# GpSimd arithmetic taken out of the routing, and the last residual spread over the experts on VectorE

## The chip, the cores and the metric

The kernel runs on one core of a Trainium2 chip. The time is the device time of one execution in microseconds (us). A core has five engines with a queue each, which run their own instructions in order and wait for each other through semaphores: TensorE (PE in the profile, its weight loads PEld), VectorE (DVE), ScalarE (ACT), GpSimd (POOL) and SyncE (SP, which only issues transfers here). TensorE's clock has two levels, 2.4 and 1.2 GHz; the profile prints the granted clock as a share of the higher one.

## The reference, cut to what matters

256 tokens of width 1024 pass a two-layer decoder: RWKV-7 time mixing and a dense SwiGLU, then dilated attention and a top-2-of-8 mixture of experts. All that matters here is the end of layer 1:

```python
def post_norm(t, y, l, j):
    gate = sub_mod[:, l, j, 2][:, None, :]
    return layer_norm(DEEPNORM_ALPHA * t + (1.0 + gate) * y, ln_g[l, j], ln_b[l, j])
...
x = post_norm(x, dilated_attention(h, k_sh, v_sh, ...), 1, 0)   # norm 1, 0
h = modulate(x, shift, scale)
top_logit, top_idx = lax.top_k((h @ router), 2)                 # routing
y = sum over experts e of  weight_e * (silu(h_e @ w_gu[e, :, :3584]) * (h_e @ w_gu[e, :, 3584:])) @ w_down[e]
x = post_norm(x, y, 1, 1)                                       # norm 1, 1
```

Each expert has 44 MB of float32 weights (1024 x 7168 and 3584 x 1024), 352 MB for all eight.

## The kernel before, in words

Tokens lie in two tiles `t` = 0 and 1 of 128 rows. Nearly all instructions come from one helper (line 191), so that a row of the profile is told apart by its tiles.

**Precision.** Every float32 weight is split in two float32r parts. `split` copies `raw` to `whi` on ScalarE (`SC.copy`) and takes `wlo = raw - whi` on VectorE; PE then makes three products a block (`mm3`: `whi` and `wlo` with the high part of the activations, `whi` with the low part). One split is 128 x 1024 elements and feeds six matmuls of 512 columns. `whi` and `wlo` have a ring of four buffers each, so ScalarE and VectorE can be up to three splits ahead of the one that PE reads. The first `GPM` splits of the experts run on GpSimd in place of VectorE: `e = GP if cnt[0] <= gp_to[0] else V`, with `gp_to[0] = cnt[0] + GPM`.

**Weights.** SP issues the loads of `raw` (1 MB each, 12 places that rotate; the first pass has a few extra places in tiles that are free by then: `lngb`, `lnbb`, `u`, `gate1`, `acc`). Loads 14, 17 and 18 (`OGP`) go through GpSimd's queue. A place is loaded again once `whi` and `wlo` have been taken from it. A line of `ln_g` or `ln_b` is loaded into `lngb` or `lnbb`, repeated on all partitions (`ln_rows`, `bcast_row`).

**Norm 1, 0 and routing** (`out_task(t)`, one for each tile). The attention's output is projected (`psb<-whi,oh` and so on), `pn_norm` makes `u = layer_norm without its row factors` on VectorE: product with the gate, residual, statistics (`bnst`, `bnmv`), a Newton root in tiny 128x1 steps (`ln_v`, `ln_i`, `ln_y`, `ln_a`), and two halves of `u`. PE transposes `u`, the modulated copy `modtmp` goes through the router (`mmb<-rt,modtmp`, 128x8), and about twenty tiny VectorE steps find the two largest logits, `oh` and `M` (one-hot), and the weights `Wt`. When both tiles are there, `route_task` counts the ranks (`mmb<-M,cnt_w`), makes the permutation `P` on VectorE, gathers the tokens of expert 0 with `P` on PE (`psb<-P,hn`), and the experts begin. At the end of `out_task` GpSimd computes the norm's row factors for the residual, which is needed much later: `yield from pn_res(t, u, pre3["gb"], pre3["bb"], GP)`, two 128x1024 products, `u<-u,lngb` and `xres<-u,lnbb`. `keep_clock2` puts dummy matmuls (`identr`) on PE where a planner at build time expects PE to wait. The order of this part is written by that planner (`spin`, from costs for each engine); in the experts the framework orders the instructions.

**Experts** (`run_experts`). Expert `i` has seven steps `j`: gate half, the down projection of the step before, up half. `macc[t]` collects the weighted outputs. In the last expert, after step 2, `moe_hook` lets GpSimd compute `macc*gate`, `xres*alpha` and their sum, so that after `fin` only the last expert's own part, the statistics and the last row factors remain.

Of the kernel before, what the change touches and what calls it, by code (L numbers as in the profile page):

```python
# [24 lines left out]
F32 = mybir.dt.float32  # L25
# [3 lines left out]
AF = mybir.ActivationFunctionType  # L29
OP = mybir.AluOpType  # L30
AX = mybir.AxisListType

D = 1024
S = 256
DFF = 2816
NE = 8
DFFE = 3584
KAPPA = math.exp(-0.5)
ALPHA = math.sqrt(2.0)
# [52 lines left out]
def tile_kernel(ctx: ExitStack, tc: tile.TileContext, cst_d, att_d, x, c, ada_w, ada_b, ln_g, ln_b, mu, w_rkv,  # L92
# [18 lines left out]
    def load(t_, src):  # L111

        n = 1
        for d_ in t_.shape:
            n *= d_
        k = t_.tensor.name
        clk["DMA"] = max(clk["DMA"], free.get(k, 0.0)) + n * 4 / 360
        rdy[k] = clk["DMA"] + 2000
        (nc.gpsimd if k in by_gp else SY).dma_start(t_, src)
# [74 lines left out]
    V, SC, GP, PE = Engine(nc.vector, "V"), Engine(nc.scalar, "SC"), Engine(nc.gpsimd, "GP"), Engine(nc.tensor, "PE")  # L194
# [216 lines left out]
    def bg_until(idx):  # L411
        while idx not in mods:
            bg_step()

    def bcast_steps(idx, o, get_ps):

        for hf in range(2):
            yield PE, mods[idx]
            ps = get_ps()
            for i in range(4):  # L420
                k = hf * 4 + i
                PE.matmul(ps[:, i * 128:(i + 1) * 128], mods[idx][:, k:k + 1].to_broadcast([128, 128]), ident,
                          start=True, stop=True)
            yield SC, ps
            SC.copy(o[:, hf * 512:(hf + 1) * 512], ps)

    def bcast_mod(idx, pool):
        bg_until(idx)
        o = pool.tile([128, D], F32, name="gate1", bufs=1)
        for _ in bcast_steps(idx, o, pst):  # L430
            pass
        return o
# [20 lines left out]
    def bcast_row(t, src):  # L453
        load(t, bass.AP(tensor=src.tensor, offset=src.offset, ap=[[0, 128], [1, t.shape[1]]]))
# [69 lines left out]
    def ln_rsqrt(var):  # L524

        v, i, y, a = (small.tile([128, 1], I32 if n == "i" else F32, name="ln_" + n, bufs=2) for n in "viya")
        yield V, var
        V.tensor_scalar(v, var, LN_EPS, -0.5, op0=OP.add, op1=OP.mult)
        yield V, v
        V.tensor_scalar(i, v.bitcast(I32), 1, None, op0=OP.logical_shift_right)  # L530
        yield V, i
        V.tensor_scalar(y.bitcast(I32), i, -1.0, float(0x5f3759df - (1 << 22) + (1 << 30)), op0=OP.mult, op1=OP.add)
        for _ in range(3):
            yield V, y
            V.scalar_tensor_tensor(a, y, v, y, op0=OP.mult, op1=OP.mult)
            yield V, a
            V.scalar_tensor_tensor(y, a, 1.5, y, op0=OP.add, op1=OP.mult)
        return y

    def pn_norm(t, yps, gate1, u, sc=(), g_=None):  # L540

        st = small.tile([128, 2, 6], F32, name="bnst", bufs=2)
        for hf in range(2):
            csl = slice(hf * 512, (hf + 1) * 512)
            yield V, yps[hf], gate1
            g = u if g_ is None else g_
            V.tensor_tensor(g[:, csl], yps[hf], gate1[:, csl], op=OP.mult)
            yield V, g, xres[0]
            V.scalar_tensor_tensor(u[:, csl], xres[0][:, t, csl], ALPHA, g[:, csl], op0=OP.mult, op1=OP.add)
            yield V, u  # L550
            V.bn_stats(st[:, hf], u[:, csl])
        mv = small.tile([128, 2], F32, name="bnmv", bufs=2)
        yield V, st
        V.bn_aggr(mv, st)
        rs = yield from ln_rsqrt(mv[:, 1:2])
        if sc:
            nm = mv[:, 1:2]
            yield V, rs
            V.scalar_tensor_tensor(nm, mv[:, 0:1], -1.0, rs, op0=OP.mult, op1=OP.mult)
        for hf in range(2):  # L560
            csl = slice(hf * 512, (hf + 1) * 512)
            if hf in sc:
                yield SC, nm
                SC.activation(u[:, csl], u[:, csl], AF.Identity, scale=rs, bias=nm)
            else:
                yield V, rs
                V.tensor_scalar(u[:, csl], u[:, csl], mv[:, 0:1], rs, op0=OP.subtract, op1=OP.mult)
# [21 lines left out]
    def pn_res(t, u, gb, bb, eng):  # L589

        yield eng, u, gb
        eng.tensor_tensor(u, u, gb, op=OP.mult)
        yield eng, u, bb
        eng.tensor_tensor(xres[0][:, t], u, bb, op=OP.add)
# [20 lines left out]
    xres = []  # L615
# [856 lines left out]
    pn = ctx.enter_context(tc.tile_pool(name="pn", bufs=1, reuse_waits="tile"))  # L1472
# [5 lines left out]
    def ln_rows(l, j):  # L1478
        gb = pn.tile([128, D], F32, name="lngb")
        bcast_row(gb, ln_g[l, j])  # L1480
        bb = pn.tile([128, D], F32, name="lnbb")
        bcast_row(bb, ln_b[l, j])
        return gb, bb
# [322 lines left out]
    lps, pre3 = {}, {}  # L1806

    def pre3_task():
        yield lambda: n_res[0] == 2 and 8 in mods
        pre3["gb"], pre3["bb"] = ln_rows(1, 0)  # L1810
        o = pn.tile([128, D], F32, name="gate1", bufs=1)
        yield lambda: banks.ok(2)
        jb = [banks.get() for _ in range(2)]
        todo = [b_[1] for b_ in jb]
        yield from bcast_steps(8, o, lambda: todo.pop(0))
        for j, _ in jb:
            banks.put(j)
        pre3["gate"] = o
        yield lambda: 9 in mods and 10 in mods
        pre3["A"], pre3["B"] = mod_ab(2, mods[10], mods[9], "m11")  # L1820
# [3 lines left out]
    def out_task(t):  # L1824
# [11 lines left out]
        bk = [banks.get((128, 512)) for _ in range(2)]  # L1836
# [7 lines left out]
        if t == 1:  # L1844
# [1 line left out]
            raw4.append(ctx.enter_context(tc.tile_pool(name="raw4", bufs=1, reuse_waits="tile")))  # L1846
            ep.append(ctx.enter_context(tc.tile_pool(name="ep", bufs=1, reuse_waits="tile")))
            xtra.extend(ep[0].tile([128, 1024], F32, name="raw", tag=tag, bufs=2) for tag in ("xeh", "xel"))
        u = pn.tile([128, D], F32, name="u", bufs=2)
        yield from pn_norm(t, [b_[1] for b_ in bk], pre3["gate"], u)  # L1850
        for j, _ in bk:
            banks.put(j)
        yield lambda: "A" in pre3 and vdone.get(1, 0) == 3
# [11 lines left out]
        for hf in range(2):  # L1865
            yield lambda: tmps.ok()
            j, ps = tr_[hf]
# [61 lines left out]
        if t == 1:  # L1929
            yield 200, SC,  # L1930
            SC.activation(tl, e2, AF.Silu)
        yield from pn_res(t, u, pre3["gb"], pre3["bb"], GP)

    mdt, mdn, hdone = {}, {}, set()

# [17 lines left out]
    macc = []  # L1953
    e_n, ep, late = [0], [], {}

    class Expert:
# [96 lines left out]
        def back(self, t):  # L2053
            for hf in range(2):
# [9 lines left out]
                else:  # L2064
                    V.scalar_tensor_tensor(macc[t][:, csl], ps, w_, macc[t][:, csl], op0=OP.mult, op1=OP.add)

    cnt_w = pn.tile([128, 2, 128], BF16, name="cnt_w")
    V.tensor_copy(cnt_w[:, 0], triS)
    GP.memset(cnt_w[:, 1], 1.0)
    route = {nm: pn.tile([128, 2, 8], BF16 if nm == "M" else F32, name=nm) for nm in ("M", "oh1", "Wt", "rank")}  # L2070
    route["n"] = 0
    alpha = pn.tile([128, 1], F32, name="alpha")
    GP.memset(alpha, ALPHA)
    experts = [Expert(m_gu[0, e], m_dn[0, e], lambda t, e=e: route["rank"][:, t, e:e + 1],
                      lambda t, e=e: route["Wt"][:, t, e:e + 1], e == 0) for e in range(NE)]

# [70 lines left out]
            banks.put(j)  # L2147

    OGP = 14, 17, 18
    DUM2, GPM, WAH = 500, 4, 4  # L2150
    AH = (0, 2, -1)
    now = clk["PE"]
    for e in clk:
# [28 lines left out]
    def run_experts(exps, hook=None):  # L2182
        prev = old = None
        if exps[0].xh is None:
            for n in range(3):
                exps[0].part(n)
        for i, e in enumerate(exps):
            for j in range(7):
                mg, mu_ = {}, {}
                if prev:  # L2190
                    mg[1] = [prev[0].tr]
                if old and j == 1:
                    mg[5] = [lambda o=old: o.back(1)]
                nxt = exps[i + 1] if i + 1 < len(exps) else None
                if nxt and j == 4:
                    for n in range(3):
                        mu_.setdefault(1 + 3 * n, []).append(lambda e=nxt, n=n: e.part(n))
                e.gate(j, mg)
                if not nxt and j == 6:
                    e.up(j, mu_)  # L2200
                if prev:
                    prev[0].down(prev[1], [e.tr] if not nxt and j == 6 else ())
                    if prev[1] == 6:
                        old = prev[0]
                        old.fin(False)
                        mu_[5] = [lambda o=old: o.back(0)]
                if nxt or j < 6:
                    e.up(j, mu_)
                prev = (e, j)
                if hook and i == len(exps) - 1 and j == 2:  # L2210
                    hook()
        e.down(6, fine=True)
        e.fin(True)
        for t in range(2):
            e.back(t)

    def moe_hook():
        late["gate"] = bcast_mod(11, pn)
        late["ln"] = ln_rows(1, 1)
        for t in range(2):  # L2220
            GP.tensor_tensor(macc[t], macc[t], late["gate"], op=OP.mult)
            GP.tensor_tensor(xres[0][:, t], xres[0][:, t], alpha.to_broadcast([128, D]), op=OP.mult)
            GP.tensor_tensor(macc[t], macc[t], xres[0][:, t], op=OP.add)

    def once(pool, tag, bufs=1):
        return lambda shape: pool.tile(list(shape), F32, name="raw", tag=tag, bufs=bufs)
# [25 lines left out]
    gb, bb = late["ln"]  # L2252
# [50 lines left out]
```

## Time and profile before

| | before |
|---|---|
| runs | 1825.33, 1828.14, 1831.77 us; median 1828.14 |
| profiled execution | 1822.58 us, span 1820.8 us |
| mean granted clock | 0.965 |
| PE busy | 1686.4 us (93%) |
| DVE busy | 1495.6 us (82%) |
| ACT busy | 1138.2 us (63%) |
| POOL busy | 268.6 us (15%) |

The span is the time from the first to the last instruction. Busy times of PE are modelled, since matmuls overlap; what an engine waited for is read from the semaphores. The attention's projection and the routing lie between about 740 and 796 us, the eight experts between 796 and 1806 us.

### The profile page before, as it was taken

The page shows a single profiled execution, that of the slowest core. Times are in us where ns is not written, and L with a number is a line of the kernel's source. Part 1 is how long each engine was busy: PE and PEld are TensorE (multiplying, and loading weights), DVE is VectorE, ACT ScalarE, POOL GpSimd, SP SyncE. Part 2 cuts the span into 40 slices and gives each one's busy share as a digit, 9 for nine tenths or more (in the row PEclk, how much of TensorE's full clock was granted, in tenths as well). Part 3 has the DMA queues.
Part 4 walks back from the last instruction along what each step waited for, and adds up shares of the span by engine and source line. Part 5 has one row for each costly group of instructions (what it writes and reads, how often), then busy time and mean ns, then how long its engine had stood idle before and what let it go on. Part 6 is the DMA issues. An engine that isn't in the chain of part 4 may idle for free. (4 is left out here: it accounts for less than half of the span.)

```text
span 1820.8 us, 26550 instructions
## 1 busy us (share of the span) xinstructions
PE 1686.4 (93%) x9876; PEld 1340.5 (74%) x9876; DVE 1495.6 (82%) x2074; ACT 1138.2 (63%) x1548; POOL 268.6 (15%) x198
## 2 busy tenths in 40 slices
PE   6998888699997889899999999999999999999896
PEld 2687656487785666688888888888788787787784
DVE  2787787799857678679898998988989888988887
ACT  2445444455544666357777777776777777777673
POOL 0011111034514875320000000000000000000200
PEclk8999989899998999979999999999999999999998
DMA  9561541299873765478999999999999999999880
GB/s 322 159 195 60 178 164 36 82 365 336 300 259 131 255 230 193 142 286 300 341 350 377 348 351 352 362 357 340 347 349 359 347 354 348 343 356 340 305 317 25
DMA packets 213566, 498.95 MB, mean 274 GB/s; under 512 B 14635, under 2 KB 28819, under 8 KB 213429
## 3 DMA queue, kind: packets, MB, share of 16 engines
q1 hardware_dynamic: 212564, 494.03, 76.4%
q0 software_dynamic: 864, 3.15, 0.5%
q8 instruction: 79, 1.29, 0.3%
q14 instruction: 59, 0.48, 0.1%
HBM read 496.07 MB, written 1.06 MB: 273 GB/s over the span
## 5 line engine op out<-in xcount | busy, mean ns | idle before, releaser
L191 DVE TENSOR_TENSOR wlo<-raw,whi 128x1024 fp32r<-128x1024 f32 x800 | 990.6, 1276 | 145.2 <-ACT whi L191 129.6
L191 ACT CAST whi<-raw 128x1024 fp32r<-128x1024 f32 x808 | 822.7, 1048 | 264.6 <-PE mmb L191 199.4
L191 PE MATMUL mmb<-wlo,xeh 128*128 128x512 f32 x896 | 356.5, 398 | 4.6 <-DVE wlo L191 3.7
L191 PE MATMUL mmb<-whi,xeh 128*128 128x512 f32 x896 | 353.0, 395 | 0.0
L191 PE MATMUL mmb<-whi,xel 128*128 128x512 f32 x896 | 352.0, 393 | 0.0
L191 PEld LDWEIGHTS mmb<-wlo,xeh 128*128 128x128 f32 x896 | 168.6, 188 | 46.8 <-DVE wlo L191 13.1
L191 PEld LDWEIGHTS mmb<-whi,xeh 128*128 128x128 f32 x896 | 168.8, 188 | 34.4 <-ACT whi L191 0.2
L191 PEld LDWEIGHTS mmb<-whi,xel 128*128 128x128 f32 x896 | 168.7, 188 | 32.7
L191 PE MATMUL psb<-wlo,ah 128*128 128x512 f32 x448 | 176.6, 394 | 1.5 <-DVE wlo L191 1.5
L191 PE MATMUL psb<-whi,al 128*128 128x512 f32 x448 | 174.8, 390 | 0.0
L191 PE MATMUL psb<-whi,ah 128*128 128x512 f32 x448 | 161.9, 391 | 0.0
L191 POOL TENSOR_TENSOR macc<-macc,gate 128x1024 f32<-128x1024 f32 x2 | 5.7, 2890 | 925.5 <-ACT gate L191 925.5
L191 POOL TENSOR_TENSOR acc<-acc,raw 128x512 f32<-128x512 f32 (+1 forms) x62 | 126.4, 2052 | 90.0 <-DVE acc L191 55.3
L191 PEld LDWEIGHTS psb<-wlo,ah 128*128 128x128 f32 x448 | 84.1, 188 | 24.8 <-DVE wlo L191 6.2
L191 PEld LDWEIGHTS psb<-whi,ah 128*128 128x128 f32 x448 | 83.5, 188 | 18.8 <-ACT whi L191 1.6
L191 PEld LDWEIGHTS psb<-whi,al 128*128 128x128 f32 x448 | 84.1, 188 | 16.4
L191 PE MATMUL mmb<-wlo,f_xh 128*128 128x512 f32 (+1 forms) x192 | 73.3, 382 | 2.3 <-DVE wlo L191 2.2
L191 PE MATMUL mmb<-whi,f_xh 128*128 128x512 f32 (+1 forms) x192 | 73.3, 383 | 1.5 <-ACT f_xh L191 1.5
L191 PE MATMUL mmb<-whi,f_xl 128*128 128x512 f32 (+1 forms) x192 | 72.4, 377 | 0.0
L191 ACT CAST ah<-psb 128x512 fp32r<-128x512 f32 x56 | 32.7, 583 | 60.9 <-PE psb L191 60.8
L191 ACT ACTIVATE e_s<-mmb 128x512 f32<-128x512 f32 x56 | 33.5, 599 | 44.9 <-PE mmb L191 44.9
L191 DVE TENSOR_TENSOR e_s<-e_s,mmb 128x512 f32<-128x512 f32 x56 | 38.3, 683 | 22.3 <-PE mmb L191 21.6
(435 smaller groups left out, 2536.3 us busy)
## 6 DMA issues: line engine op xcount, KB each, us to landing
raw<-in_moe_w_gu_dram SPq DMA_DIRECT2D x192, 1024.0 KB, 6.7
raw<-in_moe_w_down_dram SPq DMA_DIRECT2D x83, 1024.0 KB, 6.4
raw<-in_moe_w_gu_dram SPq DMA_DIRECT2D x60, 512.0 KB, 7.2
raw<-in_moe_w_down_dram SPq DMA_DIRECT2D x56, 512.0 KB, 5.9
raw<-in_ada_w_dram SPq DMA_DIRECT2D x37, 512.0 KB, 4.9
rawa<-in_ada_w_dram SPq DMA_DIRECT2D x35, 512.0 KB, 4.6
raw<-in_ada_w_dram SPq DMA_DIRECT2D x15, 1024.0 KB, 5.9
raw<-in_ffn_w_gu_dram SPq DMA_DIRECT2D x21, 512.0 KB, 5.2
```

Of the source, the lines that this page charges most:

```text
L191: return fn(*a, **kw)
```

## The change

Five things. The row factors of norm 1, 0 leave `out_task`: `u` becomes the residual tile `xres` itself, and the tile `u` is only scratch for the gate product. `GPM` is 0, so that VectorE makes the first four splits of the experts too. `moe_hook` is called after each step of each expert: after expert 1's first step it loads `ln_g`'s row into `lnbb`, and VectorE multiplies `xres` with it, a tile after each of the next two steps; the same with `ln_b` and a sum in expert 2; ScalarE multiplies by alpha in expert 3; in the last expert VectorE makes `macc*gate` and the sum with `xres`, one tile after each of steps 2 to 5. The tiles `lngb` and `lnbb` aren't loaded for norm 1, 0 any more. A pad of 128x8 takes the place of memory that a tile `alpha` and the like held.

```diff
     def pre3_task():
         yield lambda: n_res[0] == 2 and 8 in mods
-        pre3["gb"], pre3["bb"] = ln_rows(1, 0)
...
-        u = pn.tile([128, D], F32, name="u", bufs=2)
-        yield from pn_norm(t, [b_[1] for b_ in bk], pre3["gate"], u)
+        u = xres[0][:, t]
+        yield from pn_norm(t, [b_[1] for b_ in bk], pre3["gate"], u, (), pn.tile([128, D], F32, name="u", bufs=2))
...
-        yield from pn_res(t, u, pre3["gb"], pre3["bb"], GP)
...
+    pn.tile([128, 8], F32, name="pad")
...
-    alpha = pn.tile([128, 1], F32, name="alpha")
-    GP.memset(alpha, ALPHA)
...
-    DUM2, GPM, WAH = 500, 4, 4
+    DUM2, GPM, WAH = 500, 0, 4
...
-                if hook and i == len(exps) - 1 and j == 2:
-                    hook()
+                if hook:
+                    hook(i, j)
...
-    def moe_hook():
-        late["gate"] = bcast_mod(11, pn)
-        late["ln"] = ln_rows(1, 1)
-        for t in range(2):
-            GP.tensor_tensor(macc[t], macc[t], late["gate"], op=OP.mult)
-            GP.tensor_tensor(xres[0][:, t], xres[0][:, t], alpha.to_broadcast([128, D]), op=OP.mult)
-            GP.tensor_tensor(macc[t], macc[t], xres[0][:, t], op=OP.add)
+    def moe_hook(i, j):
+
+        x_, row = xres[0], late.get("row")
+        if i in (1, 2):
+            if j == 0:
+                late["row"] = pn.tile([128, D], F32, name="lnbb")
+                bcast_row(late["row"], (ln_g if i == 1 else ln_b)[1, 0])
+            if j in (1, 2):
+                V.tensor_tensor(x_[:, j - 1], x_[:, j - 1], row, op=OP.mult if i == 1 else OP.add)
+        if i == 3 and j < 2:
+            SC.activation(x_[:, j], x_[:, j], AF.Copy, scale=ALPHA)
+        if i == NE - 1:
+            if j == 1:
+                late["gate"] = bcast_mod(11, pn)
+                late["ln"] = ln_rows(1, 1)
+            if j in (2, 3):
+                V.tensor_tensor(macc[j - 2], macc[j - 2], late["gate"], op=OP.mult)
+            if j in (4, 5):
+                V.tensor_tensor(macc[j - 4], macc[j - 4], x_[:, j - 4], op=OP.add)
```

The framework places the instructions outside the routing itself, so the order is shown as built. First GpSimd's queue from the last attention work to the end of the experts (`-` before, `+` after, other rows in both; the DMA rows are its weight loads):

```order
-L191 TENSOR_TENSOR u<-u,lngb 128x1024
-L191 TENSOR_TENSOR xres<-u,lnbb 128x1024
-L191 TENSOR_TENSOR xres<-xres,alpha 128x1024
 L119 DMA raw<-in_moe_w_gu_dram 128x2x512
-L191 TENSOR_TENSOR wlo<-raw,whi 128x1024 x2
 L119 DMA raw<-in_moe_w_down_dram 128x1024
-L191 TENSOR_TENSOR wlo<-raw,whi 128x1024 x2
-L191 TENSOR_TENSOR u<-u,lngb 128x1024
-L191 TENSOR_TENSOR xres<-u,lnbb 128x1024
-L119 DMA raw<-in_moe_w_gu_dram 128x2x512 x3
-L191 TENSOR_TENSOR xres<-xres,alpha 128x1024
-L191 TENSOR_TENSOR macc<-macc,gate_15886 128x1024 x2
```

All arithmetic is gone from there, and the two pieces of load 17 now stand far ahead, where `lngb` and `lnbb` were last read in layer 0's part.

Then VectorE in the norm of tile `t` = 1, from the gate product to the variance (`BN_AGGR`), before:

```order
L191 TENSOR_TENSOR u<-psb,gate_6089 128x512
L191 SCALAR_TENSOR_TENSOR u<-xres,u 128x512
L191 BN_STATS bnst<-u 128x6
L191 TENSOR_TENSOR u<-psb,gate_6089 128x512
L191 SCALAR_TENSOR_TENSOR u<-xres,u 128x512
L191 BN_STATS bnst<-u 128x6
L191 BN_AGGR bnmv<-bnst 128x2
```

and after the change:

```order
L191 TENSOR_TENSOR u<-psb,gate_6084 128x512
L191 SCALAR_TENSOR_TENSOR xres<-xres,u 128x512
L191 BN_STATS bnst<-xres 128x6
L191 TENSOR_TENSOR wlo<-raw,whi 128x1024
L191 TENSOR_TENSOR u<-psb,gate_6084 128x512
L191 TENSOR_TENSOR wlo<-raw,whi 128x1024
L191 SCALAR_TENSOR_TENSOR xres<-xres,u 128x512
L191 TENSOR_TENSOR wlo<-raw,whi 128x1024
L191 BN_STATS bnst<-xres 128x6
L191 TENSOR_TENSOR wlo<-raw,whi 128x1024
L191 BN_AGGR bnmv<-bnst 128x2
```

The four splits that GpSimd made now stand between the steps of this norm.

Last, VectorE in the last expert after the change, where before the same stretch held only `wlo`, `e_s` (gate times up) and `al` (the low part of the activations):

```order
L191 TENSOR_TENSOR wlo<-raw,whi 128x1024 x6
L191 TENSOR_TENSOR macc<-macc,gate_15737 128x1024
L191 TENSOR_TENSOR wlo<-raw,whi 128x1024 x2
L191 TENSOR_TENSOR macc<-macc,gate_15737 128x1024
L191 TENSOR_TENSOR macc<-macc,xres 128x1024
L191 TENSOR_TENSOR e_s<-e_s,mmb 128x512
L191 TENSOR_TENSOR wlo<-raw,whi 128x1024 x2
L191 TENSOR_TENSOR al<-psb,ah 128x512
L191 TENSOR_TENSOR macc<-macc,xres 128x1024
L191 TENSOR_TENSOR wlo<-raw,whi 128x1024 x11
```

Four instructions of 128x1024 have moved in, two of them back to back ahead of `e_s`. The four on `xres` stand singly: two in expert 0 (after 38 and after 43 of its splits, since the framework draws them forward as soon as `lnbb` can be loaded) and two later.

## Rows read from the trace of the kernel before

**Rows 1.** Windows: length; PE, PEld, DVE, ACT, POOL busy; clock, DMA share, GB/s
```profile
780.00:800.00 20.00, 17.20 (x91) 16.16 (x92) 13.54 (x36) 6.61 (x13) 8.07 (x6) 0.64 0.66 250
900.00:1000.00 100.00, 100.00 (x460) 82.55 (x459) 92.13 (x87) 78.68 (x85) 0.00 (x0) 1.00 1.00 364
1700.00:1750.00 50.00, 45.41 (x197) 35.69 (x196) 42.07 (x35) 30.70 (x36) 12.41 (x4) 0.97 0.91 329
```
**Rows 2.** Waits from 800 to 1000 us: total us, times, longest
```profile
ACT whi L191 <- PE mmb L191: 25.2, 77, 1.2
...
ACT whi L191 <- DMA raw<-in_moe_w_gu_dram: 0.3, 1, 0.3
```
**Rows 3.** Waits of SP's queue from 800 to 1000 us
```profile
SPq L119 <- DVE wlo L191: 186.3, 77, 23.8
```
**Rows 4.** Timeline of POOL in the routing: start us, us
```profile
769.57 4.64 POOL L191 TENSOR_TENSOR wlo<-raw,whi 128x1024 fp32r<-128x1024 f32 x2
...
781.75 2.36 POOL L191 TENSOR_TENSOR xres<-u,lnbb 128x1024 f32<-128x1024 f32 x1
...
786.27 1.91 POOL L191 TENSOR_TENSOR xres<-xres,alpha 128x1024 f32<-128x1024 f32 x1
```
**Rows 5.** Timeline of DVE in the routing
```profile
760.10 1.78 DVE L191 SCALAR_TENSOR_TENSOR u<-xres,u 128x512 f32<-128x512 f32 x1
...
763.23 0.95 DVE L191 SCALAR_TENSOR_TENSOR u<-xres,u 128x512 f32<-128x512 f32 x1
...
764.95 0.21 DVE L191 BATCH_NORM_AGGREGATE bnmv<-bnst 128x2 f32<-128x12 f32 x1
...
765.76 8.48 DVE L191 SCALAR_TENSOR_TENSOR ln_a<-ln_y,ln_v 128x1 f32<-128x1 f32 x1
...
774.47 0.22 DVE L191 SCALAR_TENSOR_TENSOR ln_a<-ln_y,ln_v 128x1 f32<-128x1 f32 x1
...
781.80 2.33 DVE L191 TENSOR_SCALAR cnd<-cnd,e 128x8 f32<-128x8 f32 x1
...
784.31 0.16 DVE L191 TENSOR_REDUCE m<-mmb 128x1 f32<-128x8 f32 x1
...
784.97 3.25 DVE L191 TENSOR_SCALAR oh<-cnd,ix 128x8 f32<-128x8 f32 x1
...
790.21 0.48 DVE L191 TENSOR_SCALAR P<-cst,rank 128x128 f32<-128x128 f32 x2
```
**Rows 6.** Timeline of PE in the routing, idle time before in brackets
```profile
774.82 0.80 PE L191 MATMUL mmb<-identr 128*128 128x256 f32 x2 [8.70 <-DVE L L191]
...
779.25 3.42 PE L191 MATMUL mmb<-rt,modtmp 128*128 128x8 f32 x16
...
796.51 0.48 PE L191 MATMUL mmb<-whi,xeh 128*128 128x512 f32 x1
```
**Rows 7.** Timeline of POOL in the last expert
```profile
1713.65 5.73 POOL L191 TENSOR_TENSOR macc<-macc,gate 128x1024 f32<-128x1024 f32 x2 [925.48 <-ACT gate L191]
1719.35 6.71 POOL L191 TENSOR_TENSOR macc<-macc,xres 128x1024 f32<-128x1024 f32 x2
```
**Rows 8.** Timeline of DVE in the last expert
```profile
1714.56 5.91 DVE L191 TENSOR_TENSOR wlo<-raw,whi 128x1024 fp32r<-128x1024 f32 x2 [1.51 <-ACT whi L191]
```
**Rows 9.** Waits from 1712 to 1760 us
```profile
PE mmb L191 <- DVE wlo L191: 3.7, 3, 1.7
...
PE psb L191 <- DVE e_s L191: 0.8, 1, 0.8
```
**Rows 10.** Windows of tile wlo alone: PE, PEld, DVE, POOL, then as above
```profile
900.00:1000.00 100.00, 53.66 (x138) 25.84 (x138) 82.43 (x69) 0.00 (x0) 1.00 1.00 364
```
**Rows 11.** Timeline of DVE and of ACT in expert 0
```profile
820.48 1.06 ACT L191 CAST whi<-raw 128x1024 fp32r<-128x1024 f32 x1 [0.30 <-PE mmb L191]
...
832.10 10.27 DVE L191 TENSOR_TENSOR wlo<-raw,whi 128x1024 fp32r<-128x1024 f32 x8 [0.61 <-ACT whi L191]
```
**Rows 12.** Loads of lnbb: time from issue to landing
```profile
DMA to landing us min/median/max: 4.3/6.8/9.3
```

## The prediction

> **What bounds the kernel now.** I read the windows first, to see which engine has no room in which stretch. In the experts PE is busy for the whole window, VectorE 92% of it and the transfers run all the time [rows 1]: three resources near their end. The waits tell which of them leads. ScalarE waits for PE to give a `whi` buffer back before nearly every split, 77 times in 200 us, and waited once, for 0.3 us, for weights [rows 2]; SP's queue waits 186 of 200 us for VectorE to have read a `raw` place [rows 3]. So the weights come early enough, VectorE and ScalarE run as far ahead as the ring lets them, and PE sets the pace. An earlier start of the experts therefore moves the end by as much, and whatever PE loses inside them counts in full.
>
> The timelines show two places where PE loses time for another reason. In the routing PE stands idle for 8.70 us until a tiny VectorE result `L` comes [rows 6]. VectorE was not working then: one 128x1 step `ln_a` lasts 8.48 us, where its sister of the same form lasts 0.22 [rows 5]. It ends at 774.24, and GpSimd's four splits end at 774.21 [rows 4]. The same fit appears at 784.13 (`cnd`, 2.33 us) against 784.11, and at 788.22 (`oh`, 3.25 us) against 788.18 [rows 4, 5]. VectorE is held until GpSimd's arithmetic ends. In the last expert, GpSimd works 12.4 us [rows 7], two splits on VectorE take 5.91 us [rows 8] where eight took 10.27 [rows 11], and PE waits 3.7 + 0.8 us for VectorE [rows 9].
>
> **The change part by part.** A minus is a gain.
>
> *Routing, the hold before `ln_a`* goes: -(8.48 - 0.22) = -8.3 us. *The four splits* now stand in the same norm, ahead of the variance at 764.95: 4 x 10.27/8 = +5.1 [rows 5, 11]. The residual step between them took 1.78 us where its twin took 0.95 [rows 5], so -0.8. Together -4.0 for the moment at which tile 1's norm is done. The splits' inputs need ScalarE's `whi`, which it makes at the same times as before; if the fourth comes late, the bound is another +1.
>
> *The top-two search of tile 1.* Its logits end on PE at 779.25 + 3.42 = 782.67, but VectorE starts on them at 784.31, since the held `cnd` stood ahead [rows 5, 6]: -1.6. Then `oh` loses its hold: -(3.25 - 0.2) = -3.0, the 0.2 being the short steps' length. `P` follows these directly, and the experts begin at 796.51 [rows 5, 6].
>
> *The clock.* PE's long wait brings it to half speed: 0.64 granted between 780 and 800 us [rows 1], where transposes, router and gather run. With some 4 us of idleness left instead of 8.7, I expect it to fall still but to return sooner: -1.0. The ends are 0 and -4 (no half speed at all would give back up to 0.36 x 20 = 7 us of clock in that window, of which about half is work on the path).
>
> The routing gives -4.0 - 1.6 - 3.0 - 1.0 = **-9.6 us**, between -6 and -13. What it uncovers is harmless: the transfers that were queued behind the splits come earlier too, and the experts' first weights are already there.
>
> The trace is clearer on the hold than any general rule. The Trainium skill, SBUF — State Buffer, "Who interferes with whom", says that a VectorE instruction with two SBUF inputs and a GpSimd instruction that reads SBUF exclude each other for the whole of one instruction. That agrees in kind, but the row shows a hold over several GpSimd instructions in a row. By the rule as written `ln_a` would have lost one split's 2.3 us at most, and the routing would give only -9.6 + 8.3 - 2.1 = -3.4 us; I follow the row.
>
> *Last expert.* GpSimd's block goes, with PE's 4.5 us of waits [rows 9] and the fall of the clock that came with it: 0.97 over 50 us [rows 1] is 1.5 us lost. Gain -6.0. VectorE gets four products and sums of 1.28 us instead. What they cost PE depends on the lead. A split takes PE 100/69 = 1.45 us [rows 10]; when a buffer comes back, `whi` takes 1.06 and `wlo` 1.28 [rows 11] while PE has three more splits, 4.3 us, to go through. That leaves 4.3 - 2.3 = 2.0 us of spare time, less the step `e_s` or `al` that may stand in between (0.7 us). A single 1.28 fits; two back to back ahead of `e_s` (2.6 us) don't: I take +1.0, with ends at 0 and at 4 x 1.28 = +5.1. Sum **-5.0 us**, between -1 and -6.
>
> *Experts 0 to 3.* Four VectorE products and sums on `xres` stand singly and fit in the spare time; VectorE's 92% [rows 1] lets it catch up in about 16 us (8% of 16 is 1.28). Ends 0 and +5.1. The first waits for a transfer: `lnbb` is free after split 34, the product stands after split 38, about 4 x 1.45 = 5.8 us later, and such a load takes 4.3 to 9.3 us, 6.8 in the middle [rows 12]. VectorE may stand 1.0 us with splits queued behind it, 2.3 in all, just over the spare time: **+0.6**, at the worst +3. The second row is loaded long before its use. ScalarE's two products with alpha, at a split's length, lie in its waits for PE [rows 2].
>
> *At nothing:* the 1 MB of row loads that fall away and the 1 MB of expert weights that take their place in layer 0's part, both under other loads and needed much later (if not hidden, 3 us at 364 GB/s); the earlier read of the token count on SP, which now comes just before a stop for buffers; the pad.
>
> The sum is -9.6 - 5.0 + 0.6 = -14.0 us. The profiled execution took 1822.58, so it should become 1808.6; the median of the runs lies 5.6 above it, at 1828.14, and becomes **1814 us**. About 0.3% (5.5 us) is what a measurement of this kernel can tell from no change.
>
> **Rivals.**
>
> *The weight stream is the bound.* DMA is busy all the time in the experts [rows 1]. If it and not PE set the end, the earlier start would still pass on, since the loads restart when expert 0 frees its first places, but the last expert's stall would only have let the stream get ahead and would return nothing: -9.6, 1818.5 us. Against it: SP's waits for places [rows 3]. The Trainium skill, SBUF — State Buffer, "A bandwidth-pool intuition that's wrong", says that HBM, some 358 GB/s a core, is almost always the bottleneck; by that rule this is the likeliest case, and the 364 GB/s of the window stand at its figure. The waits weigh more for me. Chance 0.10.
>
> *VectorE becomes the bound of the experts.* It has 8% left. If PE has no lead over it, all eight added steps count, 10.2 us: -9.6 - 6.0 + 10.2 = -5.4, 1822.7 us. For it: PE waited for `wlo` directly in the last expert [rows 9]. Against: that was under GpSimd's hold. Chance 0.10, half of it on either side of 0.3%.
>
> *Slower: each added step falls through to PE and takes its clock along.* In the last expert the stalls cost the clock 1.5 us beside them. If each of the eight steps stalls PE by its length and costs that too, 8 x (1.28 + 1.5) = +22.2, and with `lnbb` +0.6: -9.6 - 6.0 + 22.8 = +7.2, 1835 us. It is decided from a cost of 2.6 us for each added step on (8 x 2.6 = 21, which eats 15.6 and 5.5 more). Against: the spare 2.0 us. Chance 0.05.
>
> *GpSimd isn't what holds VectorE,* and the ends agree by chance. Then only the splits' 5.1 us are left: 1833 us. Three agreements within 0.05 us speak against it. Chance 0.03.
>
> **How the numbers follow.** The forecast has 0.72, with its own range of 1808 to 1820 from the bounds above: routing -13 to -6 against the others' middle. 1807 to 1823 adds the two middle rivals and leaves out some 0.15. Faster: 0.72 + 0.10 + half of 0.10 = 0.87; same: the other half and the edge, 0.06; slower: 0.05 + the part of 0.03 that counts, 0.07.
>
> **What would show it.** In the profile after: no VectorE step of a tiny form over 0.5 us between the norm and `P`; the first `mmb<-whi,xeh` 9 to 10 us earlier, near 787; no wait of over 1.2 us of PE for `wlo` in the last expert, and no fall of the clock there; the experts between first matmul and `fin` some 4 to 5 us shorter. The prediction is wrong if the experts' stretch grows, above all around the added steps, or if the four splits make the norm of tile 1 later than the hold did.

## The result and the profile after

| | before | after |
|---|---|---|
| median of the runs | 1828.57 us (4 runs, 1825.33 to 1831.77) | 1809.4 us (4 runs, 1807.22 to 1811.16) |
| profiled execution | 1822.58 us, span 1820.8 | 1808.75 us, span 1806.6 |
| granted clock | 0.965 | 0.972 |
| POOL busy | 268.6 us | 233.4 us |

The ratio is 0.9905, 95% interval 0.9887 to 0.9923. Beside the experiments the kernel before ran 43 more times, with medians of 1826.63, 1827.19 and 1826.5 on three chips and of 1826.87 over all. So 1828.14, from which the forecast was reckoned, was some 1.3 us high, and the change is worth 0.0095 x 1827 = 17.4 us.

VectorE in the routing after the change (timeline: start, length), which answers to [rows 5]:

```profile
762.84 0.69 DVE L191 TENSOR_TENSOR u<-psb,gate 128x512 f32<-128x512 f32 x1 [1.40 <-PE psb L191]
...
771.23 0.20 DVE L191 BATCH_NORM_AGGREGATE bnmv<-bnst 128x2 f32<-128x12 f32 x1
...
772.03 0.22 DVE L191 SCALAR_TENSOR_TENSOR ln_a<-ln_y,ln_v 128x1 f32<-128x1 f32 x1
...
778.91 0.17 DVE L191 TENSOR_REDUCE m<-mmb 128x1 f32<-128x8 f32 x1 [0.47 <-PE mmb L191]
...
779.57 0.23 DVE L191 TENSOR_SCALAR oh<-cnd,ix 128x8 f32<-128x8 f32 x1
...
781.79 0.48 DVE L191 TENSOR_SCALAR P<-cst,rank 128x128 f32<-128x128 f32 x2
```

No tiny step is long any more: `ln_a` 0.22 for 8.48, `oh` 0.23 for 3.25. PE in the same place, for [rows 6]:

```profile
772.84 0.51 PE L191 MATMUL mmb<-identr 128*128 128x256 f32 x2 [3.26 <-DVE L L191]
...
776.83 2.04 PE L191 MATMUL mmb<-rt,modtmp 128*128 128x8 f32 x16
...
782.22 3.81 PE L191 MATMUL psb<-P,hn 128*128 128x128 f32 x32
...
786.00 0.48 PE L191 MATMUL mmb<-whi,xeh 128*128 128x512 f32 x1
```

The wait for `L` is 3.26 us, it was 8.70, and the router's 16 matmuls take 2.04 us, they took 3.42. The gather takes 3.81; before it was

```profile
791.34 5.20 PE L191 MATMUL psb<-P,hn 128*128 128x128 f32 x32
```

The windows (columns as in [rows 1]) say why both are faster:

```profile
760.00:780.00 20.00, 16.74 (x107) 15.31 (x106) 16.43 (x52) 8.65 (x17) 1.28 (x2) 0.91 1.04 392
780.00:800.00 20.00, 19.80 (x118) 17.04 (x117) 14.94 (x35) 13.86 (x18) 0.00 (x0) 1.00 0.39 123
...
1685.00:1735.00 50.00, 47.99 (x214) 38.29 (x213) 45.58 (x44) 34.58 (x37) 0.00 (x0) 1.00 1.04 394
```

The clock is 0.91 and then 1.00, where [rows 1] has 0.64 between 780 and 800. It still falls, but for a short while. Two windows of 5 us, the first of the kernel before, the second of the changed one:

```profile
787.00:792.00 5.00, 3.23 (x18) 3.08 (x19) 4.29 (x23) 1.69 (x3) 1.18 (x1) 0.50 1.04 390
```

```profile
772.00:777.00 5.00, 4.16 (x23) 4.16 (x23) 3.69 (x20) 0.27 (x2) 0.00 (x0) 0.66 1.04 389
```

Before, the clock was at its lower level, 0.50, from 772 to 792 us without a break; after the change it is back at 1.00 from 777 us on, as the router begins. In the last expert it stays at 1.00, and in the 50 us around the added steps PE is busy for 47.99 us, where it was for 45.41 around GpSimd's block.

To see where the time went I measure stretches from row to row: from the first gate product of tile 1 (`u<-psb,gate`, above at 762.84) to the first `mmb<-whi,xeh` is the routing, from there to the first `yh<-e_s` of the last expert (1800.6 before, 1786.6 after) the experts.

| us | before | after | change |
|---|---|---|---|
| gate product of tile 1 starts at | 759.37 | 762.84 | +3.5 |
| gate product to variance | 5.58 | 8.39 | +2.8 |
| variance to router | 14.30 | 5.60 | -8.7 |
| router to the top-two search (`m`) | 5.06 | 2.08 | -3.0 |
| search to `P` | 5.90 | 2.88 | -3.0 |
| `P` to the first expert matmul | 6.30 | 4.21 | -2.1 |
| routing in all | 37.14 | 23.16 | -14.0 |
| experts | 1004.07 | 1000.56 | -3.5 |

So the two profiles differ by 14 us only because this execution of the changed kernel came to the routing 3.5 us later; routing and experts together gave 17.5, as the runs did.

### The profile page after: what moved, and what is told of

It is laid out like the page before. It is cut to its first block, busy times and chain, and to the rows that moved or that the text cites. A ratio compares the mean times of both kernels' runs of the same rounds, so it can differ in the third digit from the quotient of the medians.

```text
span 1806.6 us, 26547 instructions
## 1 busy us (share of the span) xinstructions
PE 1682.4 (93%) x9876; PEld 1337.1 (74%) x9876; DVE 1485.7 (82%) x2086; ACT 1140.1 (63%) x1550; POOL 233.4 (13%) x183
## 5 line engine op out<-in xcount | busy, mean ns | idle before, releaser
L191 ACT ACTIVATE raw<-raw,cs_act 128x1024 f32<-128x1024 f32 x41 | 47.2, 1150 | 2.9 <-POOL ra L191 2.2
```

The costliest lines, as they stand in the source:

```text
L191: return fn(*a, **kw)
```

## The experiments

Ratios are to the kernel before, timed on the same chip; the changed kernel's is 0.9905.

**The kernel before, once more.**

> The kernel before, unchanged, for a second profile. In the profile of before the gate product of tile 1 began at 759.4 us, in those of the changed kernel and its variants at 762.0 to 764.2. Theory (the part ahead of the routing differs from one execution to the next, the change doesn't touch it): this profile has it later than 761 us, and the two stretches behind it as before, 37 us of routing and 1004 of experts. Rival (the change makes the part ahead of the routing 3.5 us longer): 759 to 760 again.

VectorE's timeline in this second profile:

```profile
764.28 0.69 DVE L191 TENSOR_TENSOR u<-psb,gate 128x512 f32<-128x512 f32 x1 [1.40 <-PE psb L191]
```

764.28, with a routing of 36.92 and experts of 1004.15 us. The part ahead of the routing varies by some 5 us, and the profile of before was an early one. A later variant of the changed kernel came to this row at 759.89. That the change costs nothing there is not shown by these few profiles, but by the runs: they gained 17.4 us, and routing and experts alone account for 17.5.

This profile shows one thing more. Its router is faster than that of the first profile (3.42 us):

```profile
784.18 2.32 PE L191 MATMUL mmb<-rt,modtmp 128*128 128x8 f32 x16
```

Still the search begins 5.1 us after the router, as before, since it waits for the held `cnd` and not for the logits.

**Splits back on GpSimd.**

```diff
-    DUM2, GPM, WAH = 500, 0, 4
+    DUM2, GPM, WAH = 500, 4, 4
```

> The changed kernel with one thing undone: the first four splits of the experts are on GpSimd again. The residual's products stay where the change put them. Theory (GpSimd's arithmetic holds VectorE): one tiny ln step of tile 1 lasts until GpSimd's fourth split ends, some 8 us. In the kernel before, the norm of tile 1 took 14.9 us from the gate product to the end of that step, in the changed one 9.4, so the first expert matmul comes 5.4 us later; if PE's long wait brings the clock to half speed again, up to 4 more. 1815 to 1819 us against 1809.4. The short steps cnd and oh of tile 1 stay short, since no residual product is on GpSimd. Rival (no hold; the splits only cost VectorE their own time): the norm is shorter by four splits, 4.5 us, 1805 us, and no tiny step is long.

1811.7 us, ratio 0.9919 (0.9903 to 0.9935); routing 26.18. GpSimd's and VectorE's timelines:

```profile
763.88 5.17 POOL L191 TENSOR_TENSOR wlo<-raw,whi 128x1024 fp32r<-128x1024 f32 x2 [9.40 <-ACT whi L191]
768.98 0.56 POOL L119 DMA_DIRECT2D raw<-in_moe_w_down_dram  x1
769.57 4.64 POOL L191 TENSOR_TENSOR wlo<-raw,whi 128x1024 fp32r<-128x1024 f32 x2
```

```profile
768.38 0.69 DVE L191 SCALAR_TENSOR_TENSOR ln_a<-ln_y,ln_v 128x1 f32<-128x1 f32 x1
768.99 0.22 DVE L191 TENSOR_SCALAR oh<-cnd,ix 128x8 f32<-128x8 f32 x1
769.12 5.11 DVE L191 SCALAR_TENSOR_TENSOR ln_y<-ln_a,ln_y 128x1 f32<-128x1 f32 x1
```

The hold is back and shows its form. `ln_a` ends at 769.07, the first pair of splits at 769.05; as GpSimd turns to a load, `oh` gets through; then `ln_y` lasts until 774.23, the second pair until 774.21. `ln_y` began 0.45 us before that pair and lasts 0.16 when it is free, so something held it already beside the load. The rival falls. But the price is 3.0 us of routing and not 5.4, and 1811.7 us lies below the expected range: the splits begin 1.8 us after the gate product here, and began 5.0 us after it before the change, since GpSimd had first to finish tile 0's residual products (its `xres<-xres,alpha` ended at 763.63). A part of the long `ln_a` was owed to those.

**The kernel before with the splits on VectorE.**

```diff
-    DUM2, GPM, WAH = 500, 4, 4
+    DUM2, GPM, WAH = 500, 0, 4
```

> The kernel before with one part of the change alone: the first four splits on VectorE. GpSimd keeps the residual's products in the routing and the block in the last expert. Theory: the 8.5 us of ln_a go, four splits of 1.2 us come in, so -4 us, and 1 to 4 us of clock with it: 1820 to 1824 us against 1828.6. The short steps cnd and oh of tile 1 still last 2 to 3 us, beside GpSimd's products. Rival one (no hold): +4.5 us, 1833. Rival two (the residual's products are what holds, the splits don't matter): no change, 1828.

1823.14 us, 0.9984 (0.9971 to 0.9998); routing 33.41, which is 3.6 less than the 37.0 of before's two profiles. VectorE, GpSimd and PE there:

```profile
779.01 2.35 DVE L191 TENSOR_SCALAR cnd<-cnd,e 128x8 f32<-128x8 f32 x1
...
782.18 3.25 DVE L191 TENSOR_SCALAR oh<-cnd,ix 128x8 f32<-128x8 f32 x1
```

```profile
778.97 2.36 POOL L191 TENSOR_TENSOR xres<-u,lnbb 128x1024 f32<-128x1024 f32 x1
781.27 2.20 POOL L119 DMA_DIRECT2D raw<-in_moe_w_gu_dram  x3
783.49 1.91 POOL L191 TENSOR_TENSOR xres<-xres,alpha 128x1024 f32<-128x1024 f32 x1
```

```profile
785.68 0.58 PE L191 MATMUL mmb<-identr 128*128 128x256 f32 x1 [5.25 <-DVE L L191]
...
788.56 4.84 PE L191 MATMUL psb<-P,hn 128*128 128x128 f32 x32
```

As the theory says, within its range. `cnd` ends at 781.36 and the product beside it at 781.33, `oh` at 785.43 and the last product at 785.40. And it parts the gain: from here to the changed kernel the routing loses another 10.3 us. Most of it lies where the residual's products hold `cnd` and `oh`, 3.0 us each; PE then waits 5.25 us, and the gather runs at a lower clock, 4.84 us for 3.81. The rest of the change goes along in this difference, so that all 10.3 are the products' is argued and not shown. Of `oh`'s 3.25 us the first 1.3 lie beside GpSimd's three loads, before the last product begins; the same stands in [rows 4, 5] (784.97 against 786.27). Whether the loads hold `oh` there was not tried.

**Routing without dummy matmuls.**

```diff
-    DUM2, GPM, WAH = 500, 0, 4
+    DUM2, GPM, WAH = 10 ** 9, 0, 4
```

> The changed kernel without the dummy matmuls on PE in the routing. Beside that the planner gives all eight modtmp pieces of tile 1 to VectorE, which is some 1 us on the path. Theory (what the prediction undersized is the clock: at half speed the same steps take longer): PE now idles from the end of tile 0's work to the transposes of tile 1, the clock falls, the router takes about 3.4 us for 2.0 and the gather 5.2 for 3.8, as in the kernel before, and the experts' first matmuls are slow until it returns: +4 to +7 us, 1813 to 1816 against 1809.4. Rival (the routing goes by VectorE's chain, PE's clock hardly matters): +1, 1810.

1813.19 us, 0.9921 (0.9906 to 0.9935); the routing is 27.50, +4.3. PE's timeline and two windows:

```profile
775.83 1.09 PE L191 MATMUL psb<-cst,xres 128*128 128x128 f32 x4 [5.90 <-DVE xres L191]
...
777.56 3.54 PE L191 MATMUL mmb<-rt,modtmp 128*128 128x8 f32 x16
...
784.63 3.75 PE L191 MATMUL psb<-P,hn 128*128 128x128 f32 x16 [1.18 <-DVE P L191]
788.17 2.40 PE L191 MATMUL mmb<-P,hn 128*128 128x128 f32 x16
```

```profile
775.00:780.00 5.00, 4.17 (x20) 4.05 (x20) 4.62 (x20) 0.20 (x1) 0.00 (x0) 0.50 1.04 388
780.00:785.00 5.00, 3.53 (x21) 3.35 (x21) 3.43 (x23) 2.62 (x5) 0.00 (x0) 0.50 0.49 193
```

After 5.9 us without work the clock is granted at 0.50, the lower level, the router is 1.5 us longer, the gather 6.15 for 3.81. With no hold at all, the clock costs these two steps 3.8 us, nearly what the prediction gave as its far end; the rest of the 4.3 is in the planner's other order. The time rose by 2.9 (ratios) to 3.8 us (medians), a little under the range.

**The four splits held back.** The first lines stand in `out_task`, behind the norm, the last in `route_task`, behind the steps that make `P`.

```diff
+        if t == 1:
+            for k in range(2):
+                V.tensor_copy(pad[:, k:k + 1], wfed[2 * NR + k][1][:, 0, 0:1].bitcast(F32))
...
-    pn.tile([128, 8], F32, name="pad")
+    pad = pn.tile([128, 8], F32, name="pad")
...
         e.slots()
+        for k in range(2, 4):
+            V.tensor_copy(pad[:, k:k + 1], wfed[2 * NR + k][1][:, 0, 0:1].bitcast(F32))
```

> The changed kernel with the first four splits of the experts kept out of the norm of tile 1: four reads of one column hold their wlo buffers, two until the norm is done, two until P is made. Theory (they stood on the path and now lie where VectorE waits for PE): gate product to variance 8.4 us becomes 3.9, the top-two search begins up to 0.7 us after its logits: -3.8 us, 1804 to 1808 against 1809.4. Rival one (the four splits were needed there, the first expert's products now wait for wlo): 0. Rival two (their raw places are loaded again 8 us later, and a later split waits for weights): +1 to +3 us.

1805.93 us, 0.9892 (0.9874 to 0.991); routing 20.20, experts 1000.45. Gate product to variance is 4.96 us for 8.39, and router to search 3.08 for 2.08. So the splits cost 3.4 us in the norm, and 3.0 of routing come back without them there. The clock doesn't fall in this routing at all (1.00 between 760 and 800 us), so that its share is in the 3.0. The intervals of the ratios overlap, so the runs alone don't show the gain; the stretches do, 20.20 to 20.22 us of routing in this kernel and in the two below that are built on it, against 23.16.

**The last expert's block on GpSimd.**

```diff
-            if j in (2, 3):
-                V.tensor_tensor(macc[j - 2], macc[j - 2], late["gate"], op=OP.mult)
-            if j in (4, 5):
-                V.tensor_tensor(macc[j - 4], macc[j - 4], x_[:, j - 4], op=OP.add)
+            if j == 2:
+                for t in range(2):
+                    GP.tensor_tensor(macc[t], macc[t], late["gate"], op=OP.mult)
+                    GP.tensor_tensor(macc[t], macc[t], x_[:, t], op=OP.add)
```

> The changed kernel with the four products and sums of the last expert on GpSimd, all after its step 2, as before the change (without the two products with alpha, which ScalarE keeps). Theory: GpSimd works some 10 us there and holds VectorE's splits. Before the change PE's starts around there fell behind by 6.4 us for 12.4 us of GpSimd's work, so 5.1 for 10; the four steps on VectorE, which fall away, cost PE 2.9 by the same count. +2.2 us, between 0 and +4: 1809 to 1813 against 1809.4. Two splits on VectorE take 5 us or more in place of 2.4. Rival (GpSimd's work is off the path, VectorE isn't held): -2.9 us, 1806.5.

1816.49 us, 0.9944 (0.9928 to 0.996); experts 1006.83, +6.3, where +2.2 and at most +4 was expected. GpSimd and VectorE (the last row is the mean, in ns, of the four splits between 1684 and 1696 us):

```profile
1683.48 5.83 POOL L191 TENSOR_TENSOR macc<-macc,gate 128x1024 f32<-128x1024 f32 x2 [912.82 <-ACT gate L191]
1689.27 6.69 POOL L191 TENSOR_TENSOR macc<-macc,xres 128x1024 f32<-128x1024 f32 x2
```

```profile
1680.24 17.94 DVE L191 TENSOR_TENSOR wlo<-raw,whi 128x1024 fp32r<-128x1024 f32 x8
```

```profile
L191 DVE TENSOR_TENSOR wlo<-raw,whi 128x1024 fp32r<-128x1024 f32 x4 | 13.4, 3409 | 0.0
```

The eight splits take 17.94 us where eight took 10.27 [rows 11], 7.7 lost to 12.5 us of GpSimd's work; I had reckoned 10, forgetting that before the change the two products with alpha weren't in this block [rows 4, 7]. The hold has another form here: while GpSimd works, VectorE makes four splits of 3.41 us each, and GpSimd's two sums take 3.35 each, where a product of this size takes 2.36 in the routing [rows 4]. No split is held for the whole block of 12.5 us; the lengths fit two engines that take turns, an instruction each. The other error is that the four steps on VectorE don't cost PE 2.9 us, as the next runs show.

**Each step of the last expert behind `e_s`, and then the last one alone.** The first holds all four back, on top of the late splits, by a tiny step that needs `e_s`; the second only the last sum; its edit is shown.

```diff
+            if j == 5:
+                V.scalar_tensor_tensor(macc[1][:, 0:1], experts[i].s[:, 0:1], 0.0, macc[1][:, 0:1], op0=OP.mult, op1=OP.add)
             if j in (4, 5):
                 V.tensor_tensor(macc[j - 4], macc[j - 4], x_[:, j - 4], op=OP.add)
```

> The kernel with the four splits held back and, in the last expert, each of the four products and sums on macc held back until its step's gate times up is done, so that they stand some 18 us apart, with nothing back to back. Theory: PE's stalls around them, 0.7 + 0.6 + 1.1 us in the changed kernel, go, since a single step fits into the lead: -2.5 us beyond the late splits, some -6.3 in all, 1803 us. Rival (each step costs PE the same wherever it stands): no difference to the late splits alone.

> The kernel with the four splits held back and, of the last expert's four steps, only the last sum held back until step 5's gate times up, so that it stands right behind that step. Theory (an added step costs PE nothing ahead of or right behind e_s, and 1.1 to 1.6 us where splits are due at once, as behind al): -1.1 us beyond the late splits alone. Rival (what it costs moves with it): no difference to the late splits.

The first: 1807.98 us, 0.9898 (0.9881 to 0.9914), experts 1003.06, 2.6 more than with the late splits alone. The expectation was wrong. PE's waits in the last expert, in the changed kernel and then in this one:

```profile
1692.62 0.66 PE L191 MATMUL psb<-cst,e_s 128*128 128x128 f32 x4 [0.55 <-DVE e_s L191]
1693.76 0.50 PE L191 MATMUL mmb<-wlo,xeh 128*128 128x512 f32 x1 [0.48 <-DVE wlo L191]
1697.76 0.50 PE L191 MATMUL mmb<-wlo,xeh 128*128 128x512 f32 x1 [0.97 <-DVE wlo L191]
```

```profile
1690.08 0.66 PE L191 MATMUL psb<-cst,e_s 128*128 128x128 f32 x4 [0.56 <-DVE e_s L191]
1691.22 0.50 PE L191 MATMUL mmb<-wlo,xeh 128*128 128x512 f32 x1 [0.48 <-DVE wlo L191]
1712.73 0.50 PE L191 MATMUL mmb<-wlo,xeh 128*128 128x512 f32 x1 [1.40 <-DVE wlo L191]
...
1748.91 0.50 PE L191 MATMUL mmb<-wlo,xeh 128*128 128x512 f32 x1 [1.40 <-DVE wlo L191]
```

The first two waits stay although no added step is near them any more: they weren't the steps' doing. Only the third was, 0.97 us, and in its place come 1.40 twice, behind the two `macc<-macc,gate` at 1709.72 and 1745.90, each of which now stands between a split and `al`. The sums, right behind `e_s`, made PE wait nowhere. So it isn't "back to back" that costs but the place. The second kernel acts on that: 1805.48 us, 0.9883 (0.9865 to 0.99), the lowest ratio of all, though its interval overlaps with that of the late splits alone; in the trace the wait of 0.97 is gone, the other two stand, and the experts take 999.74, 0.7 less than with the late splits.

**More VectorE.**

```diff
+        if i in (4, 5, 6):
+            V.tensor_tensor(x_[:, j % 2], x_[:, j % 2], x_[:, j % 2], op=OP.max)
```

> The changed kernel with 21 more VectorE steps that change no value: the maximum of xres with itself, 128 x 1024, one after each step of experts 4 to 6. They are 21 x 1.22 = 25.7 us of VectorE's time. Theory (PE sets the pace, a single added step fits into VectorE's lead): 0 to +4 us, 1809 to 1813. Rival one (VectorE is the bound of the experts): +25.7, 1835 us. Rival two (each step falls through to PE and takes clock along, 2.8 us each): +58, 1867 us.

1809.63 us, 0.9907 (0.989 to 0.9924); experts 1001.57. The framework drew the 21 steps forward to 1062 to 1237 us. That stretch in the windows, this kernel and then the changed one:

```profile
1062.00:1237.00 175.00, 174.63 (x816) 144.33 (x815) 173.99 (x169) 134.95 (x145) 0.00 (x0) 1.00 0.98 356
```

```profile
1062.00:1237.00 175.00, 175.00 (x823) 145.03 (x822) 156.84 (x149) 134.04 (x144) 0.00 (x0) 1.00 0.98 357
```

VectorE is busy 173.99 of 175 us and PE has lost next to nothing: 25.5 us of steps cost 1.0. VectorE isn't the bound, and both rivals fall; it has next to no room left there, and more steps were not tried.

**More transfers**, 21 loads of 0.5 MB, first on SP's queue, then on GpSimd's.

```diff
+        if i in (4, 5, 6):
+            load(pn.tile([128, D], F32, name="lnbb"), ada_w[0:128, j * D // 2:j * D // 2 + D])
```

```diff
+            GP.dma_start(pn.tile([128, D], F32, name="lnbb"), ada_w[0:128, j * D // 2:j * D // 2 + D])
```

> The changed kernel with 21 more loads of 0.5 MB, of weights that nothing reads, into the idle tile lnbb, one after each step of experts 4 to 6: 11 MB on top of 132. Theory (PE sets the pace; the transfers ran at 393 GB/s in one stretch of the changed kernel and at 350 in the experts' mean, so 379 with the loads still fits): 0 to +4 us, 1809 to 1813. Rival (the weight stream is the bound): 11 MB at 350 GB/s, +31 us, 1841.

> The 21 loads of 0.5 MB that nothing reads, now through GpSimd's queue, which has nothing else to do there; with that the instructions of PE, VectorE, ScalarE and SP stand in the changed kernel's order, which was not so in the run with these loads on SP's queue. The loads follow one another from expert 2's sum on, each when the one before has landed. Theory (the transfers have room): 0 to +4 us, 1809 to 1813, and a stretch of the experts at 380 GB/s or more. Rival (the stream is the bound): +31 us, 1841, and the rate stays at 350.

On SP's queue: 1832.35 us, 1.0026 (1.0012 to 1.004), experts 1024.28, which looks like the rival. But ScalarE and VectorE waited for no load in that stretch. The framework had put PE's, ScalarE's and VectorE's instructions of these experts in another order, and between 1250 and 1750 us PE waited 17.9 us for VectorE's `wlo` and `e_s`, where it waits 3.7 in the changed kernel; so this run doesn't tell the two apart. On GpSimd's queue, with the order kept: 1811.0 us, 0.9901 (0.9885 to 0.9916), experts 1000.70. The windows of this kernel and of the changed one:

```profile
1000.00:1200.00 200.00, 199.85 (x916) 164.43 (x915) 185.72 (x178) 158.76 (x170) 11.16 (x21) 1.00 1.02 386
```

```profile
1000.00:1200.00 200.00, 199.85 (x916) 164.41 (x915) 186.23 (x178) 158.45 (x169) 0.00 (x0) 1.00 0.99 360
```

386 GB/s for 360, and PE unmoved. The stream isn't the bound. The Trainium skill, SBUF — State Buffer, "A bandwidth-pool intuition that's wrong", gives some 358 GB/s and calls HBM almost always the bottleneck; 386 here and 394 in the changed kernel's last expert are above its figure, and here it isn't the bottleneck.

**No pad.**

```diff
-    pn.tile([128, 8], F32, name="pad")
```

> The changed kernel without the pad of 128x8. All instructions keep their order; only the places of later tiles move by 32 bytes a partition. Theory (nothing depends on the place): the same, 1808 to 1811. Rival (a place matters to the engines' speed): a split or matmul group with another mean duration, and over 3 us.

1822.78 us, 0.9982 (0.9967 to 0.9997): 13.4 us more, and nearly the whole gain gone. Experts 1013.03, +12.5, with the same order. First 200 us of the experts without the pad, and with it:

```profile
800.00:1000.00 200.00, 200.00 (x926) 163.38 (x925) 181.67 (x174) 153.97 (x165) 0.00 (x0) 1.00 0.94 336
```

```profile
800.00:1000.00 200.00, 200.00 (x937) 165.78 (x936) 183.00 (x175) 156.58 (x168) 0.00 (x0) 1.00 0.95 340
```

PE waits nowhere, the clock is at its higher level, and it gets through 926 matmuls where it did 937, 1.2% fewer; 1.2% of 1000 us is 12. Each matmul is slower by itself, as the means over the whole kernel (in ns, behind the comma) show, without the pad, with it and in the kernel before:

```profile
L191 PE MATMUL mmb<-whi,xeh 128*128 128x512 f32 x896 | 357.0, 399 | 0.0
```

```profile
L191 PE MATMUL mmb<-whi,xeh 128*128 128x512 f32 x896 | 352.6, 394 | 0.0
```

```profile
L191 PE MATMUL mmb<-whi,xeh 128*128 128x512 f32 x896 | 353.0, 395 | 0.0
```

So the theory is wrong: a place matters. The gain of the change isn't owed to a place, since the kernel before has 395 too; the pad keeps that. Which tile's place it is was not tried.

## Why the prediction was right, and where its sizes were off

**The hold of VectorE by GpSimd's arithmetic** is shown: it goes with the work and comes back with the splits alone, with the residual's products alone and with the last expert's block alone, for the tiny steps of the routing each time to within 0.05 us of GpSimd's ends. Over the splits it spans a run of GpSimd's instructions, 5.11 us over two of 2.3. The prediction's words "until GpSimd's arithmetic ends" are too wide, though. The residual's products hold a step for one of them at a time: `e`, shortly ahead of `cnd`, ended at 781.69 with the first product, at 781.68 (rows below), and `cnd` lasted 2.33 beside the second of 2.36 [rows 4, 5]. In the last expert the two engines take turns. The Trainium skill, SBUF — State Buffer, "Who interferes with whom", has the lock for one instruction; the rows follow it in kind, and in length for these products and the last expert, but not over the splits, where the prediction did well to go by the row. Nor is every step held. In the kernel before, GpSimd began its first pair of splits at 764.36:

```profile
764.36 4.68 POOL L191 TENSOR_TENSOR wlo<-raw,whi 128x1024 fp32r<-128x1024 f32 x2
...
779.33 2.35 POOL L191 TENSOR_TENSOR u<-u,lngb 128x1024 f32<-128x1024 f32 x1 [5.12 <-PE mmb L191]
```

```profile
780.09 1.60 DVE L191 TENSOR_TENSOR e<-e,w 128x1 f32<-128x1 f32 x1
```

`bnmv<-bnst` ran beside that pair at 764.95 in its usual 0.21 us [rows 5]; `ln_a`, which reads two tiles, is the step that stuck.

**Routing, -9.6 forecast, -14.0 measured.** The hold before `ln_a` (-8.3) and that of `oh` (-3.0) were right. The four splits were over-sized: +4.3 with the residual, measured +2.8; they add 4.5, 1.13 us each from start to start where I had reckoned 1.28, and the residual steps and the gaps around them shrink by 1.7 where I had reckoned 0.8. The term that was mis-sized most is the clock, put at -1.0: with the router's 1.4, the gather's 1.4 and the shorter steps around them it was -3.9, what is left of -14.0 without the +2.8, -8.3, -1.6, -3.0 of the other terms. I had expected the clock to fall still but to return sooner, and so it did, only much sooner, before the router and not in the gather. The run without dummies shows that the clock can move the routing by that much without any hold. Its far end of -4 was in the working, so the step is mis-sized and not mistaken. How much of the search's gain is the clock's differs between executions: by the second profile of before, whose logits end 2.8 us before the search begins and not 1.6, 1.1 of the 3.9 belong to the hold of `cnd`.

**The parts were credited unevenly.** I saw the splits as the main hold. In either order the splits are worth 3.0 to 3.6 us of routing and the residual's products 10.3 to 11.0 (37.14 to 26.18, and 33.41 to 23.16), for they delay the splits as well and keep the clock down, or in the run with the splits on VectorE bring it down again, to 0.50 between 785 and 790 us.

**Last expert and experts, -5.0 and +0.6 forecast, -3.5 measured.** The clock stayed up, as forecast. The added steps cost 0.97 us there, against 1.0, and this agreement is luck: I had put it to the two steps back to back ahead of `e_s`, which cost nothing, and it came from the single sum behind `al`. What I counted wrongly is PE's wait for `e_s`, 0.8 us [rows 9]: 0.55 of it and a 0.48 behind it are there without GpSimd, and without an added step near them. So the waits went from 4.5 to 2.0 us and not to 1.0. `lnbb` was there in time, so the 0.6 was not paid.

**At nothing:** the transfers, rightly. The pad too as it was made, but that entry hid the largest single condition of the result.

**The rivals.** Weight stream: the time of the last expert's stall was given back, and 386 GB/s fit. VectorE as the bound: no, though it stands at 99% when asked. Slower, each step falling through: one step of eight did, without the clock. No hold: no.

**The sum** of -14.0 came out at -17.5, and the base was 1.3 us too high; 1826.9 - 17.5 = 1809.4. Both errors went the same way, and the time lies near the low end of the forecast's own range. The sign that the first `mmb<-whi,xeh` would come near 787 us was met, at 786.00, by luck: the routing was 4.4 us shorter than forecast and began 3.5 us later.

## What to carry to other kernels

Where a tiny VectorE step is long and ends with GpSimd's arithmetic, take all of that arithmetic out of the stretch, not only the piece that stands beside it: it delays the next piece, and PE's waits behind both cost the clock on top. Two profiles of one pair can differ by an early part that the change doesn't touch; compare stretches from row to row, and a median over many runs. When a tile is removed, keep the addresses of what is read by the matmuls, or measure both ways.

## What the runs showed of the hardware

A shift of 32 bytes a partition made the matmuls some 1% slower, with no wait and the same clock: mean of `mmb<-whi,xel` over the kernel 395 ns for 392, of `mmb<-whi,xeh` 399 for 394. GpSimd's hold of VectorE need not let go where GpSimd issues a load between two pieces of arithmetic: in the kernel before `ln_a` lasted across such a load of 0.56 us, and with the splits back on GpSimd only `oh` and the end of `ln_a` got through. In the last expert the hold became turns, 3.41 us a split for 1.22. And a VectorE that was busy for 173.99 of 175 us kept PE busy for 174.63 of them; what made PE wait was a single step between a split and `al` (1.40 us) or right behind `al` (0.97).
